# First block: order of the query weights, the rescaling of x, the small-kernel matmul and the first attention gate

## The chip, the cores and the metric

The kernel runs on one core of a Trainium2 chip. The metric is the device time of one execution in microseconds (us). Three runs of the kernel before took 2251.32, 2252.89 and 2256.33; the median, 2252.89, is what the change is compared with. TensorE (PE) multiplies matrices, VectorE (DVE), ScalarE (ACT) and GpSimd (POOL) work on vectors, and SyncE (SP) issues most transfers.

## What is computed

Two layers of a first block and two of a second run one after the other on a sequence x of 256 rows and 1024 columns, in fp32. The change touches the first block. Cut to what matters, a layer of it is:

```python
h = rmsnorm(x, norm_mix[i])
q, k, v, cb, cc, cx, u, g = split(h @ w_in[i])      # 1024 x 5888
y_attn = sliding_window_attention(rope(q), rope(k), v) @ w_attn_o[i]
y_conv = (cb * short_conv(cc * cx, conv_w[i])) @ w_conv_o[i]
ys     = gelu(s5_ssm(u, ...))
y_ssm  = (ys * sigmoid(ys @ w_ssm_glu[i])) @ w_ssm_o[i]
gates  = sigmoid(g + b_gate[i])                     # three of 1024 columns
x = x + (gates[0]*y_attn + gates[1]*y_conv + gates[2]*y_ssm) @ w_mix_o[i]
gt, up = split(rmsnorm(x, norm_ffn[i]) @ w_ffn_in[i])
x = x + (silu(gt) * up) @ w_ffn_out[i]
```

The second block (retention, a second state space model and another gated FFN) is not changed.

## The kernel before

**Products.** x stands in SBUF transposed (features on the partitions), as a high and a low half (`xhl`) in a format that PE takes at full rate. A weight chunk of 128x1024 values comes by a transfer from SP (`raw`, L270), ACT copies its high half (`wh`, `cp`, L129) and DVE takes the difference as the low half (`wl`, `sub`, L104). Each product is three matmuls: wh with x high, wh with x low, wl with x high. `fm` (L303) makes 256 columns of output in 48 matmuls (24 where the depth is 512), `tm` (L339) makes token-major output; both take their chunks from `chunks` and `make` (L282, L291). There are 4 buffers for `raw`, 5 each for `wh` and `wl`, 4 PSUM tiles `mm` for products and 3 tiles `ax` for everything else that PE writes.

**What sets the order.** A scheduler orders the instructions of each engine by priority at build time; each engine then runs its list in order. What is written under `tc.high_priority(offset=n)` counts as if written n instructions earlier. `pinned` (L145) holds the instructions that a function adds behind the last earlier instruction of each engine; it looks for that one among the 300 instructions written last. Side work is written as generators that `bg.tick` advances at chosen places, after the tables `STEPS`, `PLAN_0` and `PLAN_1` (L22 and on).

**Start (L1574 and on).** x comes in by rows, 16 PE transposes turn it, ACT and DVE write the halves. The first norm is not applied to x at once: its row factor (`rsc`, and `rsb` along the columns) comes from sums of squares that DVE adds (`acc`), one small matmul (`st`) and a short iteration on DVE. Until x is rescaled (`Norm.rescale`, L426: multiplications by `rsb`, then new halves), results are scaled after the product.

**Layer (`layer1`, L1015).** The order is: two products for u; the product for k and v, in whose middle (`mid_kv`, L1077) the norm is finished and `spread_u` (L1038) scales both halves of u and copies them into `U2`, 16 slices of 32 partitions each, half by DVE and half by ACT; the query product; `nm.rescale`; three products for each half of the short convolution; four gates and products of the convolution's output; four gates for the ssm; then the ssm's output with the attention beside it; and for each quarter a gate of the attention, the attention's output and, at the end, the mix product, whose result goes into the next norm's sums of squares. `params_1` (called after the k and v product) turns further parameters (`vec`, `hbg`, `gfm`).

**State space model (`s5_steps`, L767).** For each of 4 groups POOL makes tables (steps A1 and A2: `BP` from `bt`, and `W` by doubling), PE and ACT transpose and copy (PC; CP further on DVE), `BXs` (L814) copies `CP` into `W` and `BP` into `BX`, `WK` (L823) transposes `BX` and multiplies it with `W` into a small kernel (`pk`, then `kk`), `KK` (L839) spreads that into `W`, and M1 and M2 apply it. In layer 0 these steps run beside the layer's products, after `PLAN_0`. The tables of layer 1 are made beside the FFN of layer 0, after `PLAN_1`; their POOL work starts while the mix product still runs, and POOL also adds the squares of the first three quarters of the mix product there.

Of the kernel before, what the change touches and what calls it, by code (L numbers as in the profile page):

```python
# [9 lines left out]
F32 = mybir.dt.float32  # L10
F32R = mybir.dt.float32r
I32 = mybir.dt.int32
AF = mybir.ActivationFunctionType
# [4 lines left out]
D = 1024  # L18
# [51 lines left out]
def body(ctx, tc, A, out):  # L70
# [60 lines left out]
    def cp(o, i, scale=None):  # L131
        return act(o, i, AF.Copy, scale=scale)
# [12 lines left out]
    def pinned(f):  # L145

        seq = nc.cur_bb.bb.instructions
        tail, last = seq[-1], {}
        for i in reversed(seq[-300:]):
            last.setdefault(i.engine, i)  # L150
        f()
        start = next(k for k in reversed(range(len(seq))) if seq[k] is tail) + 1
        for i in seq[start:]:
            if i.engine in PINNED and i.engine in last:
                tc.add_manual_dep(i, last[i.engine].name, mybir.DependencyInfo(
                    mybir.DependencyClass.NoSync, mybir.DependencyReason.DATA), reason="pinned")
# [107 lines left out]

    def chunk(parts, kn, n):

        raw, wh, wl = T(wraw, [128, 1024], "raw"), T(wsp, [128, 1024], "wh", F32R), T(wsp, [128, 1024], "wl", F32R)
        raw, wh, wl = (t[:, 0:kn * n].rearrange("p (k c) -> p k c", k=kn) for t in (raw, wh, wl))
        for ap, off in parts:
            nc.sync.dma_start(out=raw[:, :, off:off + ap.shape[1]], in_=ap.rearrange("(k p) c -> p k c", p=128))  # L270
        cp(wh, raw)
        sub(wl, raw, wh.bitcast(F32))
        return wh, wl
# [7 lines left out]

    def chunks(w, c0, K, c1=None, n=256):  # L282
        if not ahead:
            yield from make(w, c0, K, c1, n)
            return
        key, first, gen = ahead.pop(0)
        assert key == (c0, K, c1, n)
        yield from first
        yield from gen

    def make(w, c0, K, c1=None, n=256):  # L291
        KT = K // 128
        step = 2 if n == 512 else 4
        for k0 in range(0, KT, step):
            kn = min(step, KT - k0)
            rws = slice(k0 * 128, (k0 + kn) * 128)
            if c1 is None:
                parts = [(w[rws, c0:c0 + n], 0)]
            else:
                parts = [(w[rws, c0:c0 + 128], 0), (w[rws, c1:c1 + 128], 128)]  # L300
            yield k0, kn, chunk(parts, kn, n)

# [35 lines left out]

    def tm(w, c0, K, src, n=512, mid=None):  # L339

# [5 lines left out]
        KT = K // 128  # L346
        for k0, kn, (wh, wl) in chunks(w, c0, K, n=n):
            for b in range(2):
# [418 lines left out]
    def s5_steps(l, sp, wp, M=None):  # L767
# [46 lines left out]
        def BXs(b):  # L814
            W2, CP, BP = st[b]["w"][1], st[b]["CP"], st[b]["BP"]
            for ri in range(2):
                t, x = W2[:, ri], z[:, ri]
                for a in range(2):
                    r = slice(64 * a, 64 * a + 64)
                    cp(t[r, :, :, a, :], CP[r, :, ri].rearrange("p i t h -> p t i h"), -1.0 if ri else None)  # L820
                    cp(x[r, :, :, a, :], BP[r, :, ri].rearrange("p i t h -> p t i h"))

        def WK(b):  # L823
            W1, W2 = st[b]["w"][0:2]
            for ri in range(2):
                pw = axt([128, 4, 128])
                for q in range(4):
                    PE.transpose(pw[:, q, :], BX[ri][:, q, 0:128], ident)
                cp(W1[:, ri], pw)
            pk = axt([128, 128])  # L830
            for ri in range(2):
                for q in range(4):
                    mmu(pk[32 * q:32 * q + 32, :], BX[ri][:, q, 96:128],
                        W2[:, ri, q, 0:4].rearrange("p k g h -> p (k g h)"), ri == 0, ri == 1)
            kk = st[b]["kk"] = T(sp, [128, 128], "kk")
# [3 lines left out]
        def KK(b):  # L839
            KT, kk = st[b]["w"][2], st[b]["kk"]  # L840
# [78 lines left out]
    def attention(l, q_tok, k_tok, v_tok, st, acp, res):  # L919
        ap1 = st.enter_context(tc.tile_pool(name="att", bufs=1))  # L920
        ap2 = st.enter_context(tc.tile_pool(name="att2", bufs=1))
        rc = B1C[:, 384:400].rearrange("p (b e) -> p b e", b=2)
# [92 lines left out]
    def layer1(l, nm, nxt):  # L1015
# [21 lines left out]

        def spread_u(m2):  # L1038
            rsb = nm.rsb
            ps = pu[m2]  # L1040
            up = T(tmp, [128, 2, 4, 64], "ta")
            mul(up.rearrange("p f j c -> p f c j"), ps.rearrange("p f (c j) -> p f c j", j=4),
                bc(rsb.rearrange("p (c j) -> p c j", j=4), 2))
            for q in range(4):
                for j in range(4):
# [31 lines left out]
        def mid_kv():  # L1077
            nm.finish()
            for m2 in range(2):
                spread_u(m2)  # L1080

# [6 lines left out]
        bg.tick(next(steps))  # L1088
        if l == 0:
            pinned(params_1)  # L1090
        r8 = T(sm, [128, 2], "r8")
        ts(r8, nm.rsc, 0.125, None, ALU.mult, ALU.bypass)
        ps = tm(w, 0, D, XX, mid=lambda: bg.tick(next(steps)))
        for b in range(2):
            for g in range(2):
                cp(q_tok[:, b, :, g, :], ps[b][:, 256 * g:256 * g + 256].rearrange("p (m e) -> p m e", m=4), r8[:, b:b + 1])
        nm.rescale(V if l == 0 else G)
        bg.tick(next(steps))
        conv = []
        for m2 in range(2):  # L1100
            pc_ = fm(w, 1280 + 256 * m2, D, XX, mid=half)
            z = T(tmp, [128, 2, S], "ta")
            cp(z, pc_)
            bg.tick(next(steps))
            px = fm(w, 1792 + 256 * m2, D, XX, mid=half)
            mul(z, z, px)
# [11 lines left out]
            split(t, y)  # L1118
            conv.append(t)
            bg.tick(next(steps))  # L1120

        def gate(br, mp, mid=None):
            ps = fm(w, 2816 + 1024 * br + 256 * mp, D, XX, mid=mid)
            g = T(gtp, [128, 2, S], "gate")
            for k in range(2):
# [22 lines left out]
        acp = inner.enter_context(tc.tile_pool(name="acp2", bufs=2))  # L1148
        mgp = inner.enter_context(tc.tile_pool(name="mgp1", bufs=4))
        ysl = []  # L1150
        for f2 in range(2):
# [30 lines left out]
        for mp in range(4):  # L1182
            g = gate(0, mp)
            ps = fm(A["w_attn_o"][l], 256 * mp, 512, ain)
# [393 lines left out]
    g_r = ip.tile([8, 128], F32, name="g_r")  # L1578
    warm = ip.tile([128, 1], F32, name="warm")
    V.memset(warm, 0.0)  # L1580
    act(warm, warm, AF.Exp)
    nc.scalar.dma_start(out=ident, in_=A["cst"][:, C_ID:C_ID + 128])
# [69 lines left out]
```

## Time and profile before

| | us |
|---|---|
| median of 3 runs | 2252.89 |
| the profiled execution, as a run | 2256.99 |
| its span in the profile | 2255.2 |
| PE busy | 2178.6 (97%) |
| DVE busy | 1548.2 (69%) |
| ACT busy | 1221.7 (54%) |
| POOL busy | 199.6 (9%) |

The profiled execution is one run of its own; its span is the time from its first to its last instruction, 1.8 us less than the time of that run. Shares are means over the whole span. The profile's slices of a fortieth of the span show PE at 7 tenths in the first slice and in the last and at 9 or more nearly everywhere else, POOL at work in the first three, then in the fifth and sixth. The granted clock is given as a share of 2.4 GHz: 0.50 is 1.2 GHz. Its mean is 0.986.

### The profile page before, as it was taken

What the parts mean: (1) busy time and instruction counts of PE and PEld (TensorE: products, weight loads), DVE (VectorE), ACT (ScalarE), POOL (GpSimd) and SP (SyncE); (2) the same over time, 40 slices, a digit from 0 to 9 for tenths busy, and PEclk for the clock granted to TensorE, in tenths of its full rate; (3) what the DMA queues carried; (4) which work ended last, traced back from release to release, by engine and by line L of the source; (5) the groups of instructions that cost most, each with busy time, mean ns of one, the idle gap of its engine ahead of it and who ended that gap; (6) DMA issues with size and microseconds to landing.
All of it is one profiled execution on the core that took longest, in us unless ns stands there. A gap on an engine that the chain in (4) does not pass through costs nothing. (4 is left out here: it accounts for less than half of the span.)

```text
span 2255.2 us, 36864 instructions
## 1 busy us (share of the span) xinstructions
PE 2178.6 (97%) x14368; PEld 1971.0 (87%) x14368; DVE 1548.2 (69%) x2515; ACT 1221.7 (54%) x1949; POOL 199.6 (9%) x359
## 2 busy tenths in 40 slices
PE   7999969999999999999999999999999999999997
PEld 6898958899999889888999989889888899989886
DVE  7766646568756655776568887556766668887554
ACT  6666537645555444444476755444444477655442
POOL 5810244001000000100000000000100000000000
PEclk9899989999999999999999999999999999999999
DMA  6443537766645655555566646555555566456553
GB/s 184 148 127 122 168 120 240 233 207 220 195 136 178 191 186 173 162 186 165 160 201 202 187 157 192 186 174 183 171 166 177 161 200 199 149 185 196 185 178 103
DMA packets 343935, 397.75 MB, mean 176 GB/s; under 512 B 27988, under 2 KB 276688, under 8 KB 342736
## 3 DMA queue, kind: packets, MB, share of 16 engines
q1 hardware_dynamic: 342816, 394.48, 56.0%
q8 instruction: 113, 1.85, 0.3%
q10 hardware_dynamic: 592, 0.79, 0.1%
q14 instruction: 62, 0.51, 0.1%
q0 software_dynamic: 352, 0.11, 0.0%
HBM read 386.88 MB, written 8.45 MB: 175 GB/s over the span
## 5 line engine op out<-in xcount | busy, mean ns | idle before, releaser
L104 DVE TENSOR_TENSOR wl<-raw,wh 128x1024 fp32r<-128x1024 f32 (+1 forms) x698 | 850.1, 1221 | 516.5 <-ACT wh L129 488.4
L129 ACT ACTIVATE wh<-raw 128x1024 fp32r<-128x1024 f32 (+1 forms) x698 | 727.8, 1047 | 822.5 <-PE mm L135 663.4
L135 PE MATMUL mm<-xhl,wh 128*128 128x256 f32 x3616 | 672.2, 287 | 4.9 <-ACT xhl L129 3.2
L135 PE MATMUL mm<-wh,xhl 128*128 128x512 f32 (+1 forms) x2176 | 645.3, 381 | 3.0 <-DVE xhl L116 1.3
L135 PEld LDWEIGHTS mm<-xhl,wh 128*128 128x128 f32 x3616 | 567.7, 192 | 11.5 <-ACT xhl L129 4.1
L135 PE MATMUL mm<-xhl,wl 128*128 128x256 f32 (+1 forms) x1808 | 515.3, 285 | 3.8 <-DVE wl L104 3.8
L135 PEld LDWEIGHTS mm<-wh,xhl 128*128 128x128 f32 x2176 | 398.7, 190 | 81.3 <-issue 4.3
L135 PE MATMUL mm<-wl,xhl 128*128 128x512 f32 (+1 forms) x1088 | 410.4, 377 | 5.5 <-DVE wl L104 5.5
L135 PEld LDWEIGHTS mm<-xhl,wl 128*128 128x128 f32 (+1 forms) x1808 | 347.6, 192 | 5.7 <-DVE wl L104 4.9
L135 PEld LDWEIGHTS mm<-wl,xhl 128*128 128x128 f32 x1088 | 206.8, 190 | 43.2 <-DVE wl L104 6.0
L135 PE MATMUL mm<-hh,wh 128*128 128x512 f32 (+1 forms) x660 | 185.4, 348 | 0.0
L135 PE MATMUL mm<-y,wh 128*128 128x512 f32 (+1 forms) x576 | 182.1, 372 | 1.0 <-DVE y L116 1.0
L135 PE MATMUL mm<-hh,wl 128*128 128x256 f32 x528 | 147.9, 280 | 0.0
L135 PE MATMUL mm<-y,wl 128*128 128x256 f32 x512 | 144.3, 282 | 0.0
L135 PEld LDWEIGHTS mm<-hh,wh 128*128 128x128 f32 x660 | 114.7, 188 | 16.7
L135 PEld LDWEIGHTS mm<-y,wh 128*128 128x128 f32 x576 | 103.8, 188 | 21.9 <-DVE y L116 1.7
L104 POOL TENSOR_TENSOR acc<-sq 128x256 f32<-128x256 f32 x6 | 4.8, 795 | 1245.3 <-ACT sq L129 1245.3
L135 PEld LDWEIGHTS mm<-hh,wl 128*128 128x128 f32 x528 | 99.1, 188 | 0.0
L135 PEld LDWEIGHTS mm<-y,wl 128*128 128x128 f32 x512 | 96.2, 188 | 0.5 <-issue 0.3
L135 PE MATMUL mm<-mg,wh 128*128 128x256 f32 x512 | 90.5, 280 | 0.0
L135 PEld LDWEIGHTS mm<-mg,wh 128*128 128x128 f32 x512 | 78.4, 189 | 0.0
L116 DVE SCALAR_TENSOR_TENSOR ta<-mm,vec,ta 128x255 f32<-128x255 f32 (+2 forms) x144 | 67.2, 476 | 9.5 <-ACT ta L129 9.2
(363 smaller groups left out, 2446.6 us busy)
## 6 DMA issues: line engine op xcount, KB each, us to landing
raw<-in_w_in_dram SPq DMA_DIRECT2D x284, 512.0 KB, 4.3
raw<-in_w_ffn_in_dram SPq DMA_DIRECT2D x88, 512.0 KB, 3.6
raw<-in_w_gate_up_dram SPq DMA_DIRECT2D x88, 512.0 KB, 3.5
raw<-in_w_down_dram SPq DMA_DIRECT2D x42, 512.0 KB, 3.8
raw<-in_w_ffn_out_dram SPq DMA_DIRECT2D x40, 512.0 KB, 3.5
raw<-in_ret_out_dram SPq DMA_DIRECT2D x32, 512.0 KB, 3.8
raw<-in_ssd_out_dram SPq DMA_DIRECT2D x32, 512.0 KB, 3.4
raw<-in_w_mix_o_dram SPq DMA_DIRECT2D x16, 512.0 KB, 3.4
```

What stands on the lines that cost most here:

```text
L104: return eng.tensor_tensor(out=o, in0=a, in1=b, op=op)
L116: return V.scalar_tensor_tensor(out=o, in0=a, scalar=s, in1=b, op0=op0, op1=op1)
L129: return SC.activation(out=o, in_=i, func=f, **kw)
L135: return PE.matmul(out=o, lhsT=l, rhs=r, start=start, stop=stop)
```

## The change

It has these parts. (1) `pinned` looks back over 2000 instructions. (2) The query product asks for its weights 250 instructions ahead (transfer, `wh` and `wl`). (3) `BXs` copies the four parts of `BX` first, then those of `W`. (4) The small-kernel matmul moves from `WK` to `KK`, one tick later. (5) One pool of the attention gets 2 buffers. (6) `spread_u` is split: in the middle of the k and v product both halves of u are scaled, the second into free columns of `Y2`, but only the first is copied out; the second is copied after the first half of the convolution. (7) x is rescaled one product later, after the first convolution product, whose result DVE multiplies by `rsb` where ACT copied it. (8) `params_1` is called after that product. (9) The attention gates are made one step earlier each, the first ahead of the ssm output. (10) Twelve matmuls of a cleared 128x256 operand, whose result nobody reads, stand at the start of PE's list. Parts 6, 7 and 9 hold for both layers.

```diff
-        for i in reversed(seq[-300:]):
+        for i in reversed(seq[-2000:]):
...
-    def chunk(parts, kn, n):
+    def chunk(parts, kn, n, ahead_by=0):
...
-        for ap, off in parts:
-            nc.sync.dma_start(out=raw[:, :, off:off + ap.shape[1]], in_=ap.rearrange("(k p) c -> p k c", p=128))
-        cp(wh, raw)
-        sub(wl, raw, wh.bitcast(F32))
+        with tc.high_priority(offset=ahead_by):
+            for ap, off in parts:
+                nc.sync.dma_start(out=raw[:, :, off:off + ap.shape[1]], in_=ap.rearrange("(k p) c -> p k c", p=128))
+            cp(wh, raw)
+            sub(wl, raw, wh.bitcast(F32))
...
-            for ri in range(2):
-                t, x = W2[:, ri], z[:, ri]
-                for a in range(2):
-                    r = slice(64 * a, 64 * a + 64)
-                    cp(t[r, :, :, a, :], CP[r, :, ri].rearrange("p i t h -> p t i h"), -1.0 if ri else None)
-                    cp(x[r, :, :, a, :], BP[r, :, ri].rearrange("p i t h -> p t i h"))
+            halves = [(ri, a, slice(64 * a, 64 * a + 64)) for ri in range(2) for a in range(2)]
+            for ri, a, r in halves:
+                cp(z[r, ri, :, :, a, :], BP[r, :, ri].rearrange("p i t h -> p t i h"))
+            for ri, a, r in halves:
+                cp(W2[r, ri, :, :, a, :], CP[r, :, ri].rearrange("p i t h -> p t i h"), -1.0 if ri else None)
...
+        def KK(b):
+            W2, KT = st[b]["w"][1:3]
             pk = axt([128, 128])
...
-        ap2 = st.enter_context(tc.tile_pool(name="att2", bufs=1))
+        ap2 = st.enter_context(tc.tile_pool(name="att2", bufs=2))
...
-            up = T(tmp, [128, 2, 4, 64], "ta")
+            up = Y2[:, 2:4] if m2 else T(tmp, [128, 2, 4, 64], "ta")
...
-            for m2 in range(2):
-                spread_u(m2)
+            scale_u(0)
+            spread_u(0)
+            scale_u(1)
...
-        if l == 0:
-            pinned(params_1)
...
-        ps = tm(w, 0, D, XX, mid=lambda: bg.tick(next(steps)))
+        ps = tm(w, 0, D, XX, mid=lambda: bg.tick(next(steps)), ahead_by=250)
...
-        nm.rescale(V if l == 0 else G)
...
-            cp(z, pc_)
+            if m2 == 0:
+                mul(z, pc_, bc(nm.rsb, 2))
+                nm.rescale(V if l == 0 else G)
+            else:
+                cp(z, pc_)
             bg.tick(next(steps))
+            if m2 == 0 and l == 0:
+                pinned(params_1)
...
+            if m2 == 0:
+                spread_u(1)
...
+        g0 = gate(0, 0, p=inner.enter_context(tc.tile_pool(name="g0p", bufs=1)))
...
-            g = gate(0, mp)
+            g, g0 = g0, gate(0, mp + 1) if mp < 3 else None
...
-    warm = ip.tile([128, 1], F32, name="warm")
+    warm = ip.tile([128, 256], F32, name="warm")
     V.memset(warm, 0.0)
-    act(warm, warm, AF.Exp)
+    act(warm[:, 0:1], warm[:, 0:1], AF.Exp)
+    idle = axt()
+    for _ in range(12):
+        mmu(idle[:, 0, :], warm[:, 0:128], warm, True, True)
```

The order of the instructions moves in many places. Three of them follow.

ACT at the start, before, from its first work on x; `xhl` is the high half of x, cast from PSUM, `wh` the high half of the first weights, those of u:

```order
L129 ACTIVATE xhl_92<-mm_137,gfirst 128x256
L129 ACTIVATE xhl_92<-ax_138,gfirst 128x256
L129 ACTIVATE xhl_92<-mm_139,gfirst 128x256
L129 ACTIVATE xhl_92<-mm_137,gfirst 128x256
L129 ACTIVATE wh_150<-raw_149 128x1024
L129 ACTIVATE xhl_92<-ax_138,gfirst 128x256
L129 ACTIVATE xhl_92<-mm_139,gfirst 128x256
L129 ACTIVATE wh_156<-raw_155 128x1024
```

ACT at the same place, changed:

```order
L129 ACTIVATE wh_163<-raw_162 128x1024
L129 ACTIVATE wh_169<-raw_168 128x1024
L129 ACTIVATE xhl_92<-mm_150,gfirst 128x256
L129 ACTIVATE xhl_92<-ax_151,gfirst 128x256
L129 ACTIVATE wh_199<-raw_198 128x1024
L129 ACTIVATE xhl_92<-mm_152,gfirst 128x256
L129 ACTIVATE xhl_92<-mm_150,gfirst 128x256
L129 ACTIVATE xhl_92<-ax_151,gfirst 128x256
```

Two copies of weights now stand ahead of every cast of x.

DVE ahead of the query product's fourth low half, `wl_801`, before; `U_48_386` is the copied u, `CP_674` and `g` are tables of the ssm, `vec`, `hbg` and `gfm` the further parameters:

```order
L104 TENSOR_TENSOR s_p_280<-s_rv,s_cw 128x96
L104 TENSOR_TENSOR s_p_281<-s_rv,s_cw 128x96
L1051 COPY U_48_386<-ta_619 32x2x64
L104 TENSOR_TENSOR s_cw<-s_p_280,s_p_281 128x96
L1051 COPY U_48_386<-ta_619 32x2x64 x7
L218 COPY vec<-ax_689 128x128
L104 TENSOR_TENSOR g_103_736<-CP_674,s_pw 128x256
L119 TENSOR_SCALAR hbg<-vec 128x48
L104 TENSOR_TENSOR gfm<-vec 128x8
L104 TENSOR_TENSOR gf_108<-vec 128x8
L104 TENSOR_TENSOR g_104_737<-CP_674,s_pw 128x256
L104 TENSOR_TENSOR wl_801<-raw_799,wh_800 128x1024
```

DVE where the same half, now `wl_790`, stands in the change; `nt`, `nv`, `ny` are the norm's short iteration, which ends in `rsc`, the `s_` tiles tables of the ssm:

```order
L104 TENSOR_TENSOR nt_506<-nt_506,nv_503 128x2
L116 SCALAR_TENSOR_TENSOR s_r<-s_n,s_r 128x32
L116 SCALAR_TENSOR_TENSOR ny_505<-nt_506,ny_505 128x2
L119 TENSOR_SCALAR s_hs<-s_r 128x32
L104 TENSOR_TENSOR nt_506<-ny_505 128x2
L104 TENSOR_TENSOR wl_790<-raw_788,wh_789 128x1024
L116 SCALAR_TENSOR_TENSOR s_hs<-s_hs 128x32
L104 TENSOR_TENSOR nt_506<-nt_506,nv_503 128x2
L119 TENSOR_SCALAR s_hs<-s_hs 128x32
L116 SCALAR_TENSOR_TENSOR ny_505<-nt_506,ny_505 128x2
L475 COPY rsc_502<-ny_505 128x2
L119 TENSOR_SCALAR dg_522<-C,rsc_502 128x128 x2
```

The half stood behind both scalings of u and the copies; it now stands ahead of the end of the norm, on which u's scaling depends.

POOL, tables of layer 1's second group beside the mix product, before; `acc` are the additions of squares:

```order
L104 TENSOR_TENSOR g_562_3712<-W_3695,s_rot 128x64
L104 TENSOR_TENSOR g_563_3713<-W_3695,s_rot 128x64
L104 TENSOR_TENSOR W_3695<-g_562_3712,g_563_3713 128x4x8 x2
L104 TENSOR_TENSOR g_564_3718<-W_3695,s_rot 128x128
L104 TENSOR_TENSOR g_565_3719<-W_3695,s_rot 128x128
L104 TENSOR_TENSOR W_3695<-g_564_3718,g_565_3719 128x4x16 x2
L104 TENSOR_TENSOR g_566_3724<-W_3695,s_rot 128x256
L104 TENSOR_TENSOR g_567_3725<-W_3695,s_rot 128x256
L104 TENSOR_TENSOR W_3695<-g_566_3724,g_567_3725 128x4x32 x2
L104 TENSOR_TENSOR g_651_4134<-bt_3548,s_cw 128x256
L104 TENSOR_TENSOR g_652_4135<-bt_3548,s_cw 128x256
L104 TENSOR_TENSOR acc_3315<-acc_3315,sq_3453 128x256 x2
```

POOL at the same place, changed:

```order
L104 TENSOR_TENSOR W_3711<-g_560_3722,g_561_3723 128x4x4 x2
L104 TENSOR_TENSOR acc_3330<-acc_3330,sq_3468 128x256
L104 TENSOR_TENSOR g_562_3728<-W_3711,s_rot 128x64
L104 TENSOR_TENSOR g_563_3729<-W_3711,s_rot 128x64
L104 TENSOR_TENSOR acc_3330<-acc_3330,sq_3468 128x256
L104 TENSOR_TENSOR W_3711<-g_562_3728,g_563_3729 128x4x8 x2
L104 TENSOR_TENSOR g_564_3734<-W_3711,s_rot 128x128
L104 TENSOR_TENSOR g_565_3735<-W_3711,s_rot 128x128
L104 TENSOR_TENSOR W_3711<-g_564_3734,g_565_3735 128x4x16 x2
L104 TENSOR_TENSOR g_566_3740<-W_3711,s_rot 128x256
L104 TENSOR_TENSOR g_567_3741<-W_3711,s_rot 128x256
```

The two additions of the third quarter's squares stood behind the last doublings of `W` and two products with `bt`; now one stands ahead of the doubling of 128x64 and one behind its two products. The additions of the second quarter have moved ahead in the same way.

## Rows read from the trace of the kernel before

**Rows 1.** Window; busy us of PE, PEld, DVE, ACT, POOL; granted clock; DMA

```profile
0.00:330.00 330.00, 286.29 (x2114) 269.92 (x2115) 222.60 (x440) 193.86 (x382) 121.75 (x259) 0.93 0.47 144
```

**Rows 2.** Waits of PE, 0 to 330 us: total, times, longest

```profile
PE st L135 <- DVE acc L104: 16.9, 1, 16.9
PE mm L135 <- DVE wl L104: 6.7, 3, 5.5
PE ax L135 <- ACT W L129: 6.5, 3, 3.0
...
PE mm L135 <- ACT ss L129: 2.0, 1, 2.0
PE ax L828 <- ACT BX L129: 1.5, 1, 1.5
...
PE ax L941 <- DVE k_tok L104: 1.0, 1, 1.0
...
PE mm L135 <- ACT xhl L129: 0.7, 1, 0.7
```

**Rows 3.** PE's timeline in the query product: start, us, idle before

```profile
47.36 0.80 PE L135 MATMUL mm<-wl,xhl 128*128 128x512 f32 x1 [5.54 <-DVE wl L104]
```

**Rows 4.** DVE's timeline, 41 to 49 us

```profile
41.26 2.15 DVE L1051 COPY U<-ta 32x128 f32<-32x128 f32 x7
...
45.67 1.63 DVE L104 TENSOR_TENSOR wl<-raw,wh 128x1024 fp32r<-128x1024 f32 x1
...
48.10 0.68 DVE L104 TENSOR_TENSOR sq<-X,rsb 128x512 f32<-128x512 f32 x1
```

**Rows 5.** Windows of 20 to 100 us and at half clock

```profile
20.00:100.00 80.00, 68.38 (x497) 63.49 (x497) 71.80 (x168) 53.00 (x110) 64.31 (x132) 0.91 0.50 155
44.00:50.80 6.80, 3.44 (x8) 2.49 (x8) 6.38 (x12) 2.98 (x8) 6.64 (x11) 0.50 0.25 77
44.00:105.40 61.40, 51.96 (x376) 48.77 (x377) 50.25 (x71) 40.88 (x91) 57.80 (x98) 0.83 0.45 140
54.20:57.60 3.40, 3.40 (x18) 3.40 (x17) 3.40 (x6) 3.38 (x7) 3.21 (x5) 0.50 0.48 154
190.70:194.10 3.40, 3.40 (x17) 3.17 (x17) 1.23 (x1) 1.13 (x2) 0.00 (x0) 0.50 0.32 111
```

**Rows 6.** Window of the 16 transposes at the start

```profile
4.88:8.96 4.08, 4.07 (x17) 3.31 (x17) 0.91 (x3) 1.25 (x4) 2.14 (x5) 1.00 1.07 361
```

**Rows 7.** PE's timeline, first product

```profile
10.40 0.80 PE L135 MATMUL mm<-xhl,wh 128*128 128x256 f32 x2 [1.45 <-ACT wh L129]
```

**Rows 8.** Groups of PE by form: busy us, mean ns

```profile
L135 PE MATMUL ax<-qT,kT 128*128 128x256 f32 x32 | 8.2, 378 | 0.0
```

**Rows 9.** ACT's timeline at the start

```profile
10.95 1.07 ACT L129 ACTIVATE wh<-raw 128x1024 fp32r<-128x1024 f32 x1
```

**Rows 10.** ACT's timeline around the second group's BX

```profile
90.34 0.47 ACT L129 ACTIVATE W<-CP 64x320 f32<-64x320 f32 x1 [4.80 <-DVE CP L104]
...
98.30 0.42 ACT L129 ACTIVATE n<-n 128x256 f32<-128x256 f32 x1
```

**Rows 11.** PE's timeline at two small-kernel matmuls

```profile
99.35 1.08 PE L135 MATMUL ax<-W,BX 128*32 128x128 f32 x16 [3.02 <-ACT W L129]
...
153.64 0.48 PE L135 MATMUL mm<-xhl,wh 128*128 128x256 f32 x2
...
155.16 0.28 PE L135 MATMUL mm<-xhl,wh 128*128 128x256 f32 x1
157.84 0.64 PE L135 MATMUL ax<-W,BX 128*32 128x128 f32 x16 [2.40 <-ACT W L129]
```

**Rows 12.** POOL's timeline, tables of the next layer

```profile
298.12 0.40 POOL L104 TENSOR_TENSOR W<-g,g 128x16 f32<-128x16 f32 x2
...
304.62 1.52 POOL L104 TENSOR_TENSOR acc<-acc,sq 128x256 f32<-128x256 f32 x2
```

**Rows 13.** PE's timeline, transposes of q ahead of the attention

```profile
185.81 1.04 PE L947 MATMUL ax<-C,q_tok 128*128 128x128 f32 x8
```

More of the change, by code (lines that the diff above doesn't have):

```diff
@@ L280, in prefetch, with chunks @@
         ahead.append(((c0, K, c1, n), [next(gen) for _ in range(2)], gen))
-    def chunks(w, c0, K, c1=None, n=256):
+    def chunks(w, c0, K, c1=None, n=256, ahead_by=0):
         if not ahead:
-            yield from make(w, c0, K, c1, n)
+            yield from make(w, c0, K, c1, n, ahead_by)
             return
@@ L289, in chunks, with make @@
         yield from gen
-    def make(w, c0, K, c1=None, n=256):
+    def make(w, c0, K, c1=None, n=256, ahead_by=0):
         KT = K // 128
@@ L300, in make @@
                 parts = [(w[rws, c0:c0 + 128], 0), (w[rws, c1:c1 + 128], 128)]
-            yield k0, kn, chunk(parts, kn, n)
+            yield k0, kn, chunk(parts, kn, n, ahead_by)
     def fm(w, c0, K, src, c1=None, mid=None):
@@ L337, in fmb, with tm @@
         return o
-    def tm(w, c0, K, src, n=512, mid=None):
+    def tm(w, c0, K, src, n=512, mid=None, ahead_by=0):
         if n == 512:
@@ L346, in tm @@
         KT = K // 128
-        for k0, kn, (wh, wl) in chunks(w, c0, K, n=n):
+        for k0, kn, (wh, wl) in chunks(w, c0, K, n=n, ahead_by=ahead_by):
             for b in range(2):
@@ L815, in BXs @@
             W2, CP, BP = st[b]["w"][1], st[b]["CP"], st[b]["BP"]
-            for ri in range(2):
-                t, x = W2[:, ri], z[:, ri]
-                for a in range(2):
-                    r = slice(64 * a, 64 * a + 64)
-                    cp(t[r, :, :, a, :], CP[r, :, ri].rearrange("p i t h -> p t i h"), -1.0 if ri else None)
-                    cp(x[r, :, :, a, :], BP[r, :, ri].rearrange("p i t h -> p t i h"))
+            halves = [(ri, a, slice(64 * a, 64 * a + 64)) for ri in range(2) for a in range(2)]
[3 more added lines that the diff above has]
+                cp(W2[r, ri, :, :, a, :], CP[r, :, ri].rearrange("p i t h -> p t i h"), -1.0 if ri else None)
         def WK(b):
-            W1, W2 = st[b]["w"][0:2]
+            W1 = st[b]["w"][0]
             for ri in range(2):
@@ L834, in WK @@
                         W2[:, ri, q, 0:4].rearrange("p k g h -> p (k g h)"), ri == 0, ri == 1)
-            kk = st[b]["kk"] = T(sp, [128, 128], "kk")
+            kk = T(sp, [128, 128], "kk")
             cp(kk, pk)
             stt(kk[:, 0:32], eye4, dvec[:, l * 4 + b:l * 4 + b + 1], kk[:, 0:32], ALU.mult, ALU.add)
-        def KK(b):
-            KT, kk = st[b]["w"][2], st[b]["kk"]
             for q in range(4):
@@ L1036, in layer1, with scale_u, spread_u @@
             nm.step()
-        def spread_u(m2):
+        ups = []
+        def scale_u(m2):
             rsb = nm.rsb
             ps = pu[m2]
-            up = T(tmp, [128, 2, 4, 64], "ta")
+            up = Y2[:, 2:4] if m2 else T(tmp, [128, 2, 4, 64], "ta")
             mul(up.rearrange("p f j c -> p f c j"), ps.rearrange("p f (c j) -> p f c j", j=4),
                 bc(rsb.rearrange("p (c j) -> p c j", j=4), 2))
+            ups.append(up)
+        def spread_u(m2):
+            up = ups[m2]
             for q in range(4):
@@ L1119, in layer1, with gate @@
             conv.append(t)
+            if m2 == 0:
+                spread_u(1)
             bg.tick(next(steps))
-        def gate(br, mp, mid=None):
+        def gate(br, mp, mid=None, p=gtp):
             ps = fm(w, 2816 + 1024 * br + 256 * mp, D, XX, mid=mid)
-            g = T(gtp, [128, 2, S], "gate")
+            g = T(p, [128, 2, S], "gate")
             for k in range(2):
```

## The prediction

> **What bounds the kernel now.** I first read busy time by stretch [rows 1]: TensorE (PE) works 286.3 of the first 330 us, so 43.7 of its 76.6 idle us (span less the page's busy time) lie there, and the change leaves the order after them almost alone. Only this stretch is worth a count, with what the clock loses in it. The waits of PE [rows 2] name them: one of 16.9 us for DVE's sum of squares; 6.7 us for low weight halves (wl), of which 5.5 in one piece; 6.5 us in three pieces for W; 2.0 for ss, 1.5 for BX, 1.0 for k_tok, 0.7 for xhl. The timelines then say why. The 5.54 us piece stands inside the query product [rows 3]: its fourth wl starts on DVE at 45.67 only, behind copies of u (seven of them alone take 2.15 us) and the parameter work [rows 4]; until it came, PE stood. After waits the granted clock falls from 2.4 to 1.2 GHz: it reads 0.50 at 44.0 to 50.8, 54.2 to 57.6 and 190.7 to 194.1, and PE worked 3.44, 3.40 and 3.40 us in them [rows 5]. Half of such work is time lost. The last row of that group, DVE 71.8 busy of 80 us from 20 to 100, is the warning: there DVE is nearly as full as PE could be.
>
> **The change part by part**, gains counted positive.
>
> *Start.* Before, 16 transposes and one small one took 4.07 us [rows 6] and PE's first product started at 10.40 [rows 7]. (The clock column reads 1.00 there, but 0.25 for a transpose is half the pace of later ones.) Now 12 full-precision matmuls of 128x256 run ahead of the transposes. The only such shape in the trace shows 32 records in 8.2 us, 0.256 each [rows 8]; I count two records for one matmul, so 24, or 6.1 us at full clock and up to 12.3 at half. Begun soon after the operand is cleared, at some 1.2 us by my estimate, they would end between 7.5 and 13.5; I take 9 to 10, since the clock should rise within them. The 16 transposes then cost 2.1 us. But two weight copies now stand ahead of all casts of x on ACT, so the first cast starts after the second copy, which before started at 10.95 and took 1.07 [rows 9], and without casts ahead of it may start near 10; so x is ready near 11.2 and the u products begin at 11.6 rather than 10.4, at full clock if the warming works. Their end I put at 26 to 27 against 26.0: the norm's sum of squares is also later by some 4 us and its matmul sits 12 matmuls before that end. **Term -0.7**, from +1.5 (everything warm) to -3.
>
> *Query weights and rescale.* In the new order all four wl of the query precede rsc on DVE, so the 5.54 wait goes. With it go 0.67 for xhl, 0.66 for the next wl and half of 3.44 + 3.40 us: 10.3 at most. But DVE does the same work less eight u copies (about 2.2) and plus one multiplication, since the first conv product is read by a scaled multiplication on DVE (0.68, as the product of x and the same row takes [rows 4]) instead of an ACT copy. So new waits follow: the broadcast of rsc about 0.5 late; the first conv weights now sit behind u's second scaling and two table products, 2.0; the first use of the rescaled x, which still needs a cast and a subtraction after the product before it, 1.0; the wl behind the eight scaled slices and the parameter copy, 2.2. 10.3 - 5.7 = **4.5**, from 0 to 10.
>
> *Small-kernel matmul.* The copies into BX no longer stand behind W<-CP on ACT; that ACT waited until 90.34 for DVE's CP [rows 10], so the 1.5 us wait goes. The small-kernel matmul waits 6.5 us in three pieces [rows 2], 3.02, 2.40 [rows 11] and the 1.05 left over: the row names W, but its PSUM slot is released by DVE's last read of the sum before, which follows the ACT step at 98.30 [rows 10]. It now has 24 matmuls between itself and the transposes instead of 13 to 15. Twelve such matmuls started in 1.52 us [rows 11], 0.127 each. For the first wait nothing upstream becomes faster but ACT's order (about 0.5), so the gain is 9 x 0.127 + 0.5 = 1.6: what the BX wait gives, the later wait takes back. I take **1.5** (0 to 5, if the half clock there goes too). For the second, 11 x 0.127 = 1.4 covers all of 1.05; for the third the same 1.4 leaves 1.0, less a weight copy that leaves ACT's chain. **2.5**.
>
> *ssm output.* The gate product of 48 matmuls, 48 x 0.127 = 6.1 us, now runs ahead of the first ss matmul, and the transposes of k and q come 24 matmuls after. The waits of 2.0 and 1.0 [rows 2] are covered three times over, and the half-clock stretch behind them (half of 3.40) should go: **4.7**, at least 3. Each later gate is one step earlier, which covers part of the short attention waits: **0.5**.
>
> *The sum of squares.* PE idles 16.9 us because POOL holds the squares' additions of the third pair behind the tables of the next layer: they run 304.62 to 306.14 [rows 12]. With the longer look back they stand behind the additions of 298.12 instead, one before and one after the next product pair. The remaining 4 steps of tables no longer precede them: end near 300.6, **5.5**. PE still waits some 11 us there and still comes back at half clock. The bound below is 0 (another input arrives late, squares come from ACT), above 6.5.
>
> *Layer two of this block, FFN, second block.* The same rescale on POOL, a step later, finds about as much cover; the small-kernel matmul in the FFN had no wait. **0**, plus or minus 1. A second attention buffer frees no wait that the trace shows: 0.
>
> **Sum**: -0.7 + 4.5 + 1.5 + 2.5 + 4.7 + 0.5 + 5.5 = 18.5 us. The profiled execution took 2256.99, so 2238.5 for such a one; the median of the runs is 4.1 lower, 2252.89, so **2234.4**. A measurement of this kernel can tell about 0.2%, 4.5 us, from no change.
>
> **The rivals.**
>
> *DVE is the bound until 100 us.* For it: 71.8 busy of 80 [rows 5], and the third point at which PE meets DVE, the small-kernel matmul at 99.35 [rows 11], takes back whatever PE wins before it unless DVE comes earlier as well. Against it: 8.2 us of idle DVE, and the eight copies that leave. Then the terms 4.5 and 1.5 are nothing and the late start (-3) is carried on: 18.5 - 4.5 - 1.5 - 2.3 = 10.2, **2242.7**. Chance 0.18.
>
> *Everything comes out.* Start +1.5, query 10, first BX and small kernel 4.5 with its half clock, third wait whole (+0.9), a later dip of the clock gone (+1.5): 18.5 + 2.2 + 5.5 + 3 + 0.9 + 1.5 = 31.6, **2221.3**. Against it stands DVE's load. Chance 0.12.
>
> *Slower: the clock stays low.* One wait of 5.5 us becomes four or five short ones on wl, dg and xhl between 32 and 100 us. Short waits sufficed for a drop: it came at 190.7 after one of 1.0 and one of 2.0 [rows 2, 5]. From 44.0 to 105.4 the mean granted clock was 0.83 [rows 5], that is (1 - 0.83) x 61.4 / 0.5 = 21 us at half clock, and PE worked 52. If PE kept 1.2 GHz through it, the other 40 us would last about 20 longer, against 12.5 from the start and the later terms: 8 slower, **2261**. It decides from the point at which some 46 of those 61 us are at half clock. Against it: with the waits a quarter as long, the clock rose again each time within some 7 us. Chance 0.07.
>
> *The warmth is lost again in the transposes.* In this trace eight transposes in a row, coming from a busy stretch, took 1.04 us [rows 13], 0.13 each, the full rate; at the start each took double [rows 6], coming from nothing. So the trace shows that they can run at 2.4 GHz, not that the clock survives sixteen of them and a pause until x is ready. If it does not, idle matmuls that end at 9.5 only push the transposes back, those take 4.1 us, and the u products start at about 13.7 at half rate: -5 at the start in place of -0.7, **2238.7**. Chance 0.1. The Trainium skill, "TensorE: Matmul & The Clock Gate", Part 4: PE-mode transpose, says that the full clock does not engage for transposes; by that the start would be this rival's -5, though the row of eight speaks against it as a general rule.
>
> **How the numbers follow.** The forecast has 0.53, the rivals 0.18, 0.12, 0.07 and 0.10. The range 2222 to 2246 leaves out the slower case (0.07), half of the best (0.06) and the worse part of the first rival (0.05). Faster by over 0.2% means under 2248.4: all but the slower case and a part of the first rival. Faster 0.88, same 0.05, slower 0.07.
>
> **What would show it.** In the new profile: no wait over 2.5 us on wl between 30 and 60 us; DVE idle under 6 us from 20 to 95; first u product at 11 to 12 us with matmuls 0.12 apart at once; a small-kernel wait of 2 to 4 us left near 92; no wait before ss; the sum of squares' wait 11 to 12 us, with POOL's last addition two thirds of the way through the tables. The forecast is wrong if PE's idle time in the first 330 us does not fall by over 12 us, or if the clock reads 0.5 for more than 40 us there.

## The result, and the profile after

The changed kernel took **2241.19 us** (median of 4 runs, 2239.88 to 2241.91); the kernel before, run beside it, 2254.61 (2251.32 to 2256.79). The ratio is 0.9941, 95% interval [0.9924, 0.9958]: 13.4 us less. The forecast was 2234.4 and its range 2222 to 2246. The time lies in the range; the parts it was made of did not come out as forecast.

| profiled execution | before | after |
|---|---|---|
| time, us | 2256.99 | 2241.91 |
| span, us | 2255.2 | 2240.1 |
| PE busy in the first 330 us [rows 1] | 286.29 | 292.61 |
| granted clock there | 0.93 | 0.95 |
| start of the sum-of-squares matmul | 307.12 | 300.10 |
| from there to the end | 1948.1 | 1940.0 |

The last two rows part the profile's 15.1 us: 7.0 arise ahead of the matmul of layer 0's sum of squares and 8.1 behind it. Behind it stand the FFN of layer 0, then layer 1, in which parts 2, 6, 7 and 9 of the change hold too, and then work that the change leaves as it is. The next two sums of squares on PE part these, first before, then after:

```profile
508.43 0.50 PE L135 MATMUL st<-C,acc 128*128 128x1 f32 x4
...
740.24 0.50 PE L135 MATMUL st<-C,acc 128*128 128x1 f32 x4
```

```profile
501.44 0.50 PE L135 MATMUL st<-C,acc 128*128 128x1 f32 x4
...
733.28 0.50 PE L135 MATMUL st<-C,acc 128*128 128x1 f32 x4
```

The FFN took 201.3 us in both, layer 1 took 231.8 in both. So the change won nothing in layer 1, as the prediction's term of 0 has it, and the 8.1 us lie behind 740 us, in unchanged work. They are taken up under before_again.

PE's waits in the first 330 us after the change, to be read against [rows 2]: what was waited for, then total, times, longest.

```profile
PE st L135 <- DVE acc L104: 13.2, 1, 13.2
PE mm L135 <- DVE wl L104: 10.6, 4, 7.2
PE mm L135 <- ACT xhl L129: 7.9, 1, 7.9
...
PE ax L135 <- POOL g L104: 0.7, 1, 0.7
```

The waits for W, ss, BX and k_tok have left the list, as forecast. But wl waits longer than before (10.6 against 6.7), and one for xhl of 7.9 us is new. Where they stand, by PE's timeline (start, duration, instruction, count, idle before it and what ended that):

```profile
59.88 1.10 PE L135 MATMUL mm<-xhl,wh 128*128 128x256 f32 x2 [7.94 <-ACT xhl L129]
...
68.18 0.39 PE L135 MATMUL mm<-xhl,wl 128*128 128x256 f32 x1 [2.29 <-DVE wl L104]
...
92.71 0.58 PE L135 MATMUL mm<-xhl,wl 128*128 128x256 f32 x1 [7.17 <-DVE wl L104]
...
300.10 1.01 PE L135 MATMUL st<-C,acc 128*128 128x1 f32 x4 [13.16 <-DVE acc L104]
```

The first stands at the second convolution product, the first to use the rescaled x, the second within the same product, the third in a later one. The windows of after (columns as in [rows 1]) show what the engines did meanwhile:

```profile
56.70:63.50 6.80, 3.62 (x15) 3.39 (x16) 3.64 (x7) 6.74 (x14) 6.21 (x23) 0.50 0.00 0
90.80:97.60 6.80, 4.89 (x23) 4.89 (x24) 6.80 (x12) 3.47 (x7) 0.00 (x0) 0.50 0.49 140
292.20:305.90 13.70, 5.80 (x16) 4.74 (x17) 6.43 (x17) 0.00 (x0) 13.04 (x31) 0.50 0.22 61
40.00:60.00 20.00, 11.29 (x73) 10.01 (x71) 11.14 (x26) 9.66 (x21) 18.71 (x50) 0.92 0.26 79
60.00:80.00 20.00, 17.71 (x144) 16.93 (x145) 19.83 (x35) 12.32 (x27) 18.86 (x36) 0.91 0.29 85
```

At the end of each of the three long waits and behind it the clock reads 0.50, that is 1.2 GHz, for 6.8, 6.8 and 13.7 us; PE worked 3.62, 4.89 and 5.80 us of these. From 40 to 60 DVE works 11.1 of 20 us, ACT 9.7 and POOL 18.7; from 60 to 80 DVE works 19.8. So DVE first stands idle and then has no idle time left to catch up in.

**Why the 7.94 us.** ACT's timeline in that stretch:

```profile
53.14 0.84 ACT L129 ACTIVATE BX<-BP 64x256 f32<-64x256 f32 x2 [7.88 <-POOL BP L104]
54.00 1.06 ACT L129 ACTIVATE wh<-raw 128x1024 fp32r<-128x1024 f32 x1
55.08 0.84 ACT L129 ACTIVATE q_tok<-mm,r 128x256 f32<-128x256 f32 x2
...
59.32 1.71 ACT L129 ACTIVATE xhl<-sq,gfirst 128x256 fp32r<-128x256 f32 x4
```

ACT runs its instructions in order, and 7.88 us of idle time stand before a copy into BX, whose input POOL had not made. Behind that copy stand a weight copy, the four scaled copies of q, the other copies into BX and those into W and, at 59.32, the cast of the rescaled x. DVE waits for the cast in turn, with 8.61 us idle:

```profile
34.48 1.09 DVE L104 TENSOR_TENSOR ta<-mm,rsb 128x512 f32<-128x512 f32 x1 [0.69 <-ACT rsb L129]
35.41 0.17 DVE L119 TENSOR_SCALAR s_u<-s_x 128x32 f32<-128x32 f32 x1
...
49.98 1.27 DVE L104 TENSOR_TENSOR wl<-raw,wh 128x1024 fp32r<-128x1024 f32 x1
59.86 1.96 DVE L116 SCALAR_TENSOR_TENSOR xhl<-sq,gfirst,xhl 128x256 fp32r<-128x256 f32 x4 [8.61 <-ACT xhl L129]
```

POOL is late for two reasons. Its chain needs the second s_u, which DVE now makes at 35.41, behind the scaling of u (before at 31.35); of these 4.1 us, 2.4 are that rsc itself comes later (32.70 for 30.35). And the chain takes longer. POOL after the change, with a low half that DVE makes beside it, and then POOL before:

```profile
35.68 0.29 POOL L104 TENSOR_TENSOR c<-s_u 128x32 f32<-128x32 f32 x1 [1.75 <-DVE s_u L119]
...
44.72 1.27 DVE L104 TENSOR_TENSOR wl<-raw,wh 128x1024 fp32r<-128x1024 f32 x1
...
44.99 1.49 POOL L104 TENSOR_TENSOR c<-s_rot 128x32 f32<-128x32 f32 x2
...
52.38 0.72 POOL L104 TENSOR_TENSOR BP<-g,g 128x256 f32<-128x256 f32 x1
```

```profile
31.34 0.53 POOL L104 TENSOR_TENSOR c<-s_u 128x32 f32<-128x32 f32 x2 [21.36 <-issue]
...
40.52 0.47 POOL L104 TENSOR_TENSOR c<-s_rot 128x32 f32<-128x32 f32 x2
...
43.98 0.79 POOL L104 TENSOR_TENSOR BP<-g,g 128x256 f32<-128x256 f32 x1
```

The second `c` starts 4.1 us later (35.68 for 31.61), and from there to BP the same instructions take 16.7 us instead of 12.4; so BP comes 8.4 us later. The instructions that grew stand from 44.1 us on, where DVE works at wl, `g`, CP and sq: the two products at 44.99 took 1.49 us beside a wl, and 0.47 before, where no wl was being made. That DVE's work is what slows them is read from this overlap; no run tests it by itself. Before, ACT waited 1.64 us for BP.

The 7.17 us wait at 92.71 comes of DVE's fullness from 60 us on, as ACT's timeline and then DVE's show:

```profile
88.28 0.63 ACT L129 ACTIVATE ac<-tb 128x512 fp32r<-128x512 f32 x1 [2.72 <-DVE tb L104]
88.81 1.04 ACT L129 ACTIVATE wh<-raw 128x1024 fp32r<-128x1024 f32 x1
```

```profile
88.11 1.81 DVE L104 TENSOR_TENSOR m<-m,W 128x512 f32<-128x512 f32 x2
...
91.44 1.21 DVE L104 TENSOR_TENSOR wl<-raw,wh 128x1024 fp32r<-128x1024 f32 x1
```

The wh of that product stands on ACT behind a cast that had waited 2.72 us for DVE, and its wl on DVE behind the steps of the recurrence.

**Theory.** The gate that runs ahead carries the net gain. The early parts lose at ACT's queue, in the one place (BX behind POOL), what they win elsewhere. **Rivals:** DVE is the bound until 100 us whatever ACT does; or the early parts carry part of the gain.

### The profile page after: what moved, and what is told of

Its sections match the earlier page's. It is cut to its first block, busy times and chain, and to the rows that moved or that the text cites. A ratio compares the mean times of both kernels' runs of the same rounds, so it can differ in the third digit from the quotient of the medians.

```text
span 2240.1 us, 36899 instructions
## 1 busy us (share of the span) xinstructions
PE 2174.7 (97%) x14392; PEld 1967.3 (88%) x14392; DVE 1547.9 (69%) x2517; ACT 1221.7 (55%) x1947; POOL 198.8 (9%) x359
## 5 line engine op out<-in xcount | busy, mean ns | idle before, releaser
L135 PEld LDWEIGHTS mm<-xhl,wh 128*128 128x128 f32 x3616 | 566.1, 192 | 16.7 <-ACT xhl L129 10.5
L135 PEld LDWEIGHTS mm<-hh,wh 128*128 128x128 f32 x660 | 114.7, 188 | 16.7
```

What stands on the lines that cost most here:

```text
L135: return PE.matmul(out=o, lhsT=l, rhs=r, start=start, stop=stop)
```

## The experiments

Every kernel is compared with the kernel before run on the same chip; brackets after a ratio are its 95% interval. "Start of st" is the start of the sum-of-squares matmul in the run's profile (before 307.12, after 300.10), a mark that what lies behind cannot disturb; between two profiles of one kernel it still moved by up to 3.1 us (279.63 and 276.53, below). Differences to the change are of medians from different chips, on which the kernel before took 2254.27 to 2255.91.

**gate_late**: the change without the gate that runs ahead.

```diff
-        g0 = gate(0, 0, p=inner.enter_context(tc.tile_pool(name="g0p", bufs=1)))
-            g, g0 = g0, gate(0, mp + 1) if mp < 3 else None
+            g = gate(0, mp)
```

> The changed kernel with the attention gates made where they were before (first gate behind the ssm output, none a step early); everything else as changed. In the build this also puts the squares' additions of the third quarter on POOL back behind the tables. Theory (the gate move carries nearly the whole gain, the first 165 us none): the waits on k_tok and ss of 1.0 and 2.0 us and the half clock behind them return (about 5.5 us) and the wait for the sum of squares grows from 13.2 to about 16.5, so 2249 to 2251 against 2241.2 for the changed kernel. Rival (the query, the start and the small kernel carry it): 2241 to 2244.

Measured: 2253.52 us, 0.9992 [0.9977, 1.0006]; start of st 308.34. Its waits of PE:

```profile
PE st L135 <- DVE acc L104: 18.2, 1, 18.2
...
PE mm L135 <- ACT xhl L129: 6.5, 1, 6.5
...
PE mm L135 <- ACT ss L129: 2.0, 1, 2.0
PE ax L941 <- DVE k_tok L104: 1.0, 1, 1.0
```

Without the gate the rest of the change is worth nothing that can be told; the time is above even the theory's range. The waits for ss and k_tok are back, and so is that for the sum of squares, at 18.2 us for 16.9 before: POOL's last additions stand together again, at 305.84. So the move of POOL's additions belongs to the gate.

**gate_only**: the kernel before with the gate's lines and nothing else.

```diff
-        def gate(br, mp, mid=None):
+        def gate(br, mp, mid=None, p=gtp):
-            g = T(gtp, [128, 2, S], "gate")
+            g = T(p, [128, 2, S], "gate")
+        g0 = gate(0, 0, p=inner.enter_context(tc.tile_pool(name="g0p", bufs=1)))
-            g = gate(0, mp)
+            g, g0 = g0, gate(0, mp + 1) if mp < 3 else None
```

> The kernel before with the gate move alone (first attention gate ahead of the ssm output, each later one a step early); nothing else changed. In the build POOL's additions of squares move with it. Theory (the gate move carries the whole gain): 2240 to 2244, the sum of squares' matmul at 298 to 300 us as in the changed kernel (300.1), and the waits on ss and k_tok gone. Rival (gate and early parts share it): 2246 to 2249.

Measured: 2246.97 us, 0.9963 [0.9948, 0.9978]; the profiled execution took 2240.76 and was the fastest of nine (up to 2251.14). By the median the rival's range held. By the profile the theory did: st starts at 297.11, 10.0 ahead of the kernel before and 3.0 ahead of the full change.

```profile
PE st L135 <- DVE acc L104: 13.1, 1, 13.1
PE ax L135 <- ACT W L129: 7.0, 3, 4.1
PE mm L135 <- DVE wl L104: 6.4, 3, 5.6
```

The waits for W and wl are there, those for ss and k_tok are not, and the sum of squares waits 13.1 us, as after the full change. What the early parts add to it is -3.0 us at st and +5.8 by the medians: not settled by this pair.

**bx_late**: the change with the first group's BX a step later in the plan, so that ACT's queue no longer meets it ahead of the cast.

```diff
-PLAN_0 = ("A1:0 A2:0", "PC:0 A1:1", "CP:0 A2:1", "", "BX:0", "", "WK:0",
+PLAN_0 = ("A1:0 A2:0", "PC:0 A1:1", "CP:0 A2:1", "", "", "BX:0", "WK:0",
```

> The changed kernel with the first group's copies into BX planned one tick later, so that ACT casts the rescaled x before it waits for POOL's BP. Theory (the new 7.9 us wait on xhl is ACT standing in its own queue behind BX, for which POOL's BP came 8 us later than before): that wait falls under 2 us and DVE's idle 8.6 us at 51 to 60 goes; 2235 to 2237, if no later wait takes it back. Rival (DVE is the bound until 100 us, as in the prediction's first rival): the wait moves to low weight halves behind, 2240 to 2242.

Measured: 2233.36 us, 0.9907 [0.9889, 0.9925], 7.8 under the change; start of st 289.12, 11.0 earlier. The waits of PE, and where the cast and BX now stand on ACT:

```profile
PE st L135 <- DVE acc L104: 13.2, 1, 13.2
PE mm L135 <- DVE wl L104: 3.8, 3, 2.0
PE ax L135 <- ACT W L129: 3.4, 1, 3.4
PE mm L135 <- DVE xhl L116: 3.2, 3, 2.8
```

```profile
50.30 1.69 ACT L129 ACTIVATE xhl<-sq,gfirst 128x256 fp32r<-128x256 f32 x4
...
59.75 1.70 ACT L129 ACTIVATE BX<-BP 64x256 f32<-64x256 f32 x4
```

The cast starts 9.0 us earlier. The 7.9 and the 7.2 us are both gone, so the second followed from the first; 2.8 us of wait on xhl, now for DVE's half, are left where under 2 were expected. The gain is a little over the theory's. This is the run against the rival that DVE was the bound: with one step of the plan moved, and no work taken from DVE, most of the early loss comes back. DVE then works 19.8 of the 20 us from 40 to 60 and 19.7 from 60 to 80.

**kk_in_wk**: the change with the small-kernel matmul back where it was, a step earlier (the pk block of KK moved into WK, kk handed on).

```diff
         def WK(b):
...
+            pk = axt([128, 128])
...
+            kk = st[b]["kk"] = T(sp, [128, 128], "kk")
...
         def KK(b):
+            KT, kk = st[b]["w"][2], st[b]["kk"]
-            W2, KT = st[b]["w"][1:3]
-            pk = axt([128, 128])
...
```

> The changed kernel with the small-kernel matmul back in WK, directly behind the transposes. Theory (the extra matmuls between them cover waits of 1 to 3 us): the waits on W return, 1.0, 2.4 and about 3 us, 2243 to 2246. Rival (these waits only moved; what PE wins there it loses at the next meeting with DVE): 2240 to 2242.

Measured: 2244.92 us, 0.9961 [0.9947, 0.9976]; start of st 301.97. Three waits ahead of small-kernel matmuls are there (1.3, 1.3 and 0.9 us, shorter than expected), where the change has one of 0.7. The move is worth 3.7 us by the medians, 1.9 at st; forecast 4.0. The intervals of the two ratios overlap, so the size of this is not settled.

**no_idle**: the change without the 12 matmuls at the start.

```diff
-    idle = axt()
-    for _ in range(12):
-        mmu(idle[:, 0, :], warm[:, 0:128], warm, True, True)
```

> The changed kernel without the twelve idle matmuls; the build then casts x ahead of the weights' copies again, as before the change. Theory (the idle matmuls win nothing: the u products end 0.9 us later than before): 2239 to 2241.5. Rival (they keep the clock up and without them the start loses its half-clock products): 2243 to 2245.

Measured: 2242.99 us, 0.9953 [0.9935, 0.9971]; start of st 297.37. In the profile it is 2.7 us ahead at st, in the medians 1.8 behind: the matmuls' worth is under what can be told here.

**before_again**: the kernel before, unchanged, for a second profile.

> The kernel before, once more with a profile. From the matmul of the sum of squares (st, 307.1 us) to the end it took 1948.1 us, the changed kernel 1940.0, though the order of instructions there is the same. Theory (that stretch varies from run to run by some us, with its own short waits and clock drops): this look gives another length, 1940 to 1950, with the dips near 952, 1611 and 1938 us not all at the same places. Rival (the change reaches behind 330 us): 1947 to 1949, with all three dips.

Measured: 2250.10 us, start of st 307.69, and 1940.6 us from there to the end, where the first profile has 1948.1 with the same program. Part of that the clock shows: in the first profile it reads 0.50 near 952, 1611 and 1938 us, in this one at none of the three. The first place, in the first profile and in this one:

```profile
951.90:955.30 3.40, 3.40 (x9) 2.64 (x10) 3.40 (x6) 0.94 (x3) 1.98 (x2) 0.50 0.00 0
```

```profile
950.00:956.00 6.00, 5.02 (x22) 3.79 (x22) 6.00 (x12) 3.08 (x6) 2.44 (x2) 1.00 0.01 3
```

The expectation has the order behind st as the same; in layer 1 it is not, but layer 1 took 231.8 us in both kernels. From its sum of squares to the end the first profile of the kernel before took 1515.0 us, this one 1507.8 and the change 1506.8. So the 8.1 us behind st are little more than what two profiles of one program differ by.

**acc_dve**: the change with all of the squares' additions on DVE.

```diff
-            eng = V if mp == 3 or self.gain is gfirst else G
+            eng = V
```

> The changed kernel with all additions of the mix product's squares on DVE instead of POOL. Theory (PE's 13.2 us wait for the sum of squares is POOL's queue of tables and nothing else): the wait falls to 1 to 2 us and the half clock behind it goes (some 3 us), 2226 to 2230 against 2241.2. Rival (something else is late just behind it, the FFN's weights or the norm's chain): PE waits on over 5 us there, 2233 to 2238.

Measured: 2224.88 us, 0.9871 [0.9854, 0.9887], 16.3 under the change, more than expected. The wait is not shortened but gone, and the clock stays at 1.00 where it read 0.50 for 13.7 us:

```profile
287.22 0.50 PE L135 MATMUL st<-C,acc 128*128 128x1 f32 x4
```

```profile
287.00:307.00 20.00, 20.00 (x95) 16.66 (x94) 18.07 (x35) 12.03 (x20) 18.95 (x35) 1.00 0.61 186
```

PE works all of the 20 us, and DVE, at 18.1 of 20, had the room. The 13.2 us wait hung on POOL alone.

**gate_acc_dve**: gate_only with the edit of acc_dve (`eng = V`), so that only the early parts stand between it and acc_dve.

> The kernel before with the gate move and the additions of squares on DVE, and none of the early parts. Theory (the early parts as they stand are worth nothing, and are worth 8 us or more only with the BX copies a tick later): 2229 to 2232, some 14 above the 2216.1 of the version with all of them and the later BX. Rival (the later BX only repairs what the early parts broke, and they win nothing at all): 2215 to 2219.

Measured: 2227.62 us, 0.9877 [0.9859, 0.9894]; start of st 286.04. The early parts as they stand are worth 2.7 us by the medians and -1.2 at st: nothing that can be told, as the theory has it, though the time is below its range.

**bx_late_acc_dve** and **best_again**, one kernel run twice: both edits, BX a step later and the additions on DVE.

```diff
-PLAN_0 = ("A1:0 A2:0", "PC:0 A1:1", "CP:0 A2:1", "", "BX:0", "", "WK:0",
+PLAN_0 = ("A1:0 A2:0", "PC:0 A1:1", "CP:0 A2:1", "", "", "BX:0", "WK:0",
-            eng = V if mp == 3 or self.gain is gfirst else G
+            eng = V
```

> Both edits on the changed kernel: the first group's copies into BX planned one tick later, the additions of squares on DVE. Theory (the two waits lie in different stretches and add): 2241.2 - 7.8 - 13 = 2218 to 2222. Rival (one of them gives back what the other wins): over 2226.

> The version with both edits and with the idle matmuls, once more, beside the next run on the same chip. If they keep something: 2214 to 2218 and 3 us or more below the next run. If the difference of 4 us seen before is spread: within 2 us of it. In either case the sum of squares' matmul near 279.6 us.

Measured: 2216.08 us, 0.9832 [0.9816, 0.9849], and 2215.77, 0.9821 [0.9808, 0.9835]; start of st 279.63 and 276.53. This beats both kernels, by about 39 and 25 us. The two gains add: 7.8 and 16.3 us singly, 25.1 together. The theory, which had 13 for the second, was some 2 us too high. Against gate_acc_dve the early parts with the later BX are worth 11.5 and 11.9 us; no run has the later BX without the early parts, so how the two share this is not shown. The second profile's st is 3 us ahead of the first's and of its expectation. The waits of best_again until 330 us, and its window of 20 to 95:

```profile
PE mm L135 <- DVE wl L104: 5.9, 3, 3.8
...
PE ax L135 <- POOL BP L104: 2.7, 1, 2.7
```

```profile
20.00:95.00 75.00, 68.00 (x513) 62.62 (x512) 72.71 (x172) 54.74 (x112) 57.24 (x111) 0.98 0.55 168
```

Here DVE is busy 72.7 of 75 us: the bound that the first rival named is likely the next one, now that ACT's queue is free. No run takes work from DVE there.

**best_no_idle** and **no_idle_again**, one kernel run twice: the same with the three lines that no_idle deletes left out as well.

> The version with both edits (BX copies a tick later, additions of squares on DVE) without the twelve idle matmuls. Without them the sum of squares' matmul of the mix product came 2.7 us earlier in one look (297.4 against 300.1), yet the timed median was 1.8 us later, which is within the spread. Theory (they win nothing, and their delay of the u products and of the norm costs some 2 us): 2212 to 2216 against 2216.1. Rival (they do keep something): 2218 to 2220.

> The same version without the idle matmuls, once more. If they keep something: 2218 to 2222. If spread: 2214 to 2218. The sum of squares' matmul near 275.9 us, so that whatever they keep must lie behind it.

Measured: 2220.05 us, 0.9843 [0.9828, 0.9858], and 2217.69, 0.9831 [0.9817, 0.9844]; start of st 275.89 and 276.44. In every comparison of these, no_idle's included, the kernel with the matmuls is 1.6 to 4.3 us faster by the medians and no earlier at st. The two pairs of expectations point to opposite sides (2220.05 lies in the rival's range, 2217.69 in that of spread). Their worth stays open.

## Why the prediction was right in its total and wrong in its parts

By the marks on PE, from the profiles of before and after. A mark is the start of the same instruction in both (for u, the end); the gain of a part is the growth of the lead between two marks:

| part | mark at its end, before → after | forecast | found |
|---|---|---|---|
| start | end of u's products, 26.02 → 26.96 | -0.7 | -0.9 |
| query weights and rescale | second group's transposes, 91.96 → 103.10 | +4.5 | -10.2 |
| small-kernel matmul | last group's product of xs ahead of the attention, 176.01 → 177.69 | +4.0 | +9.5 |
| ssm output | transposes of o, 230.65 → 232.74, with 5.8 us of a gate already done | +4.7 | +5.4 |
| later gates | begin of the wait for the sum of squares, 290.17 → 286.94 | +0.5 | -0.5 |
| sum of squares | its matmul, 307.12 → 300.10 | +5.5 | +3.8 |
| sum | | 18.5 | 7.0 |

**The step that failed is "Query weights and rescale".** It let the 5.54 us wait go, which was right, and priced four new waits at 0.5, 2.0, 1.0 and 2.2, together 5.7. They measured 0.77, 7.94, 2.29 and 7.17, together 18.2, and with them came two stretches at half clock in which PE worked 3.62 and 4.89 us, which the term left out. The broadcast of rsc cost PE nothing, the first conv weights 0.77 for 2.0, the first use of the rescaled x 7.94 for 1.0, the wl behind the slices 2.29 for 2.2, and the 7.17 were not in it. What it lacked is POOL's BP at the head of ACT's queue. Scaling u in front of the second s_u was seen as a load on DVE and not as the start of POOL's chain, and that chain was taken to run at its old pace: it started 4.1 us later and took 4.3 longer. In no_idle it starts only 1.2 us later than before (32.50 for 31.34), yet BP comes 4.1 later and xhl still waits 7.2, so the later start is not all of it. "The first use of the rescaled x" was costed as a cast and a subtraction; the cast stood behind the copies of BX, wh, q_tok and W on ACT. bx_late shows it: 7.8 us back, 11.0 at st, by moving one entry of the plan.

**Small-kernel matmul.** What the runs show is in line with the mechanism: in place of 1.05 and 2.40 us of wait stand 0.72 and none, and kk_in_wk gives 3.7 for undoing it. That the lead grows by 9.5 in this part is the other side of the loss before it: PE arrives late, and what it waited for in [rows 11] is ready; so the 2 to 4 us that were to be left there are not. The two parts together are -0.7 against +8.5 forecast.

**ssm output** came out as worked out (5.4 for 4.7). gate_late shows both waits back, of 2.0 and 1.0 us.

**Sum of squares.** The gain came (3.8 for 5.5), by another cause than the one named. It was put down to "the longer look back". In gate_only that look back is the old one and the wait is 13.1 us; in gate_late it is the new one and the wait is 18.2. The gate ahead moves the products by which POOL's additions are placed. With the old look back the changed kernel's program is the same, instruction by instruction, on PE, DVE, ACT and POOL, so part 1 of the change does nothing in it. PE's wait that remained was 13.2 us where 11 to 12 were forecast.

**Start.** -0.9 for -0.7, but by other numbers than forecast, so the hit is luck: a later begin and a faster product cancel. The idle matmuls began at 2.74 instead of 1.2, since ACT's Exp on the same tile comes first. They took 8.5 us, as forecast, and so ended at 11.2, not 9 to 10. The first matmul of u came at 13.0, not 11.6, and the steady pace of 0.12 us each only from 15.4, after short waits:

```profile
2.74 8.47 PE L135 MATMUL ax<-warm 128*128 128x256 f32 x24 [2.74 <-ACT warm L129]
...
11.29 0.65 PE L1614 MATMUL mm<-C,xin 128*128 128x128 f32 x4
12.66 0.60 PE L1614 MATMUL ax<-C,xin 128*128 128x128 f32 x4
13.02 0.36 PE L135 MATMUL mm<-xhl,wh 128*128 128x256 f32 x1
```

**The rivals.** That warmth is lost in the transposes falls: the 16 of them took 11.29 to 13.02, 0.11 each, against 0.25 before [rows 6], and the products behind ran at full pace. The Trainium skill, "TensorE: Matmul & The Clock Gate", Part 4: PE-mode transpose, says that the full clock does not engage for transposes; the trace differs: the 16 from 11.29 to 13.02 are its measure. Whether transposes alone raise the clock no run here tests. The first rival gave 2242.7, nearer to the 2241.19 than the forecast, with its two terms at nothing and the late start carried on. Its reason, that DVE is full, holds from 60 us only; from 40 to 60 DVE had 8.9 us idle, and bx_late won without taking work from it. The clock did not stay low: the mean from 44 to 105.4 rose from 0.83 to 0.89.

**What was to show it wrong** did. PE's idle time in the first 330 us fell by 6.3 us (43.7 to 37.4) where over 12 were asked, and DVE was idle 11.2 of the 75 us from 20 to 95 where under 6 were asked. No wl waited over 2.5 us between 30 and 60, as asked, but xhl did. That the time is in the range is in part luck: the gain of 7.0 us taken from 2254.61 would be 2247.6, outside the range. The rest came, by the profiles, behind 740 us, where the forecast had nothing and two profiles of one program differ by 7. Of the 13.4 us by the medians 7.0 are accounted for in the first block; whether the change has a part in the other 6 stays open.

## What to carry to other kernels

When work is moved ahead on one engine, follow the queue of each helper engine behind it: an in-order engine that meets a copy too early holds up everything behind the copy, and the wait shows up on PE under another name (here xhl, for POOL's BP). Ask of every small instruction that is pushed back whose chain it starts and what that chain will then run beside: 4 us at its start became 8 at its end. And build each part of a change alone before crediting it: the order showed that the move of POOL's additions came with the gate, not with the edit that seemed to be meant for it.

## What the runs showed of the hardware

A matmul of 128x256 in full precision ran at 0.353 us per record at the start (24 records in 8.47 us), between the 0.256 of [rows 8] and twice that. The granted clock behind st fell to 0.50 for 3.4 us in three places in one execution of the kernel before (951.9, 1610.7, 1938.3) and in none of these in another execution of the same program; at the first of them PE worked 3.40 of 3.40 us, so by estimate a dip of this kind costs half of it, some 1.7 us. Two profiles of one kernel therefore differ by more than some of the parts of this change are worth, and a mark ahead of the remainder (the start of st) parted the two where the end time alone could not.

In the changed kernel two of POOL's products of 128x32 took 1.49 us at 44.99, beside DVE's subtraction of two SBUF tiles of 128x1024, and 0.45 us at 43.15, beside DVE's product of 128x512 that reads one operand from PSUM. So it matters for POOL's pace what DVE does beside it; these are single places of one trace.
